# Decoder layer with stick-breaking attention, mLSTM and PEER experts: gate tables beside the next attention, transposed attention weights, and a last pass that ranks one block first

## The chip, the cores and the metric

One NeuronCore of a Trainium2 chip runs the whole layer in one launch. The metric is the device time of that launch in microseconds (us); lower is better. All data are float32.

## The reference, cut to what matters

1024 tokens of width 1024 go through one layer. The kernel works on eight token blocks of 128.

```python
h = layer_norm(x, ln0)
# token mixer: one input projection feeds both branches
z = (q @ k.T) / 8                                   # 8 heads of 64, causal, s < t
w = exp(log_sigmoid(z) + sum_{s'>s} log_sigmoid(-z))  # stick-breaking weights
o_sb = w @ v
o_ml = sigmoid(ml_o) * mlstm(silu(conv(ml_q, ml_k)), ml_v, gates)   # 4 heads of 128
h = layer_norm(ALPHA*h + (sigmoid(g1)*(o_sb @ Wsb) + sigmoid(g2)*(o_ml @ Wml)) @ w_out, ln1)
# PEER: 8 heads; each token takes 16 of 16384 experts per head
s1, s2 = q1 @ k1.T, q2 @ k2.T                       # 128 scores each, per head
v1, i1 = top_k(s1, 16); v2, i2 = top_k(s2, 16)
top_s, pos = top_k(v1[:, None] + v2[None, :], 16)   # out of 256 pairs
idx = (i1*128 + i2)[pos]; gates = softmax(top_s)
ffn = sum_k gates_k * gelu(h . u_tab[idx_k]) * v_tab[idx_k]
h = layer_norm(ALPHA*h + ffn + sigmoid(h @ Wg) * (p @ Wp), ln2)
```

## The kernel before, in words

**Passes.** `BLOCKS` cuts the eight token blocks into three passes, (0, 1), (2, 3, 4) and (5, 6, 7), which `main` (L1141) runs one after the other. A pass is: `pre` (first layer norm and transposes), `project` (L478: keys and values of the attention to DRAM, queries to SBUF), `attention` (L552) merged with `recurrent`, `mlstm` and `gates`, then `branch` (L747: branch projections, output projection, second layer norm), `keys` (L810: the PEER scores and, for each of 16 head halves, the top 16 by `best`, L802), `choose` (L873: pair sums, top 16 pairs, expert numbers, softmax) and `embed` (L839). `pre`, `project` and `embed` of neighbouring passes are merged with these.

**Experts, two ways.** For blocks 0, 1, 2, 5 and 6 class `Experts` (L1063) gathers expert rows: POOL issues one indirect DMA for each of the 128 choices of a block (128 rows of 4 KB into one tile `vr`, `K` = 6 of them, L1078), first from `u` (`first`; VectorE multiplies and sums, L1099), then from `v` (`second`; VectorE adds, L1111). This is 1280 gathers and 1280 VectorE steps over the run. It goes on beside everything from the first `choose` to the end. `first` of one block and `second` of the block before take turns; the loop at L1165 hands one such step to the program for each 1.15 of the cost that `main` yields. Blocks 3, 4 and 7 (`DENSE`) go through all 16384 experts in `dense` (L1009): 128 steps of 24 + 6 matmuls, with gates from tables `Gd` in DRAM that `spread` (L954) makes. `spread` builds one-hot matrices `ohA` and `ohB` on VectorE and ScalarE for four tokens at a time, multiplies them on TensorE and copies the product into `stage` tiles, which SP stores in 16 pieces of 512 KB for each block.

**Attention.** An item is one row (head pair `pr`, token block `j`, head `e` of the pair) by up to four key blocks; rows of blocks 4 to 7 have two items. `s1`: scores (64 of 128 partitions are contracted), then Abs, Exp, Ln and Relu on ScalarE. `s2`: a running sum from the right on VectorE (L597), subtracted from the scale times the scores (L599), then Exp. `s3`: one transpose of each 128x128 piece on TensorE and a copy to `awT`. `s4`: weights by values, 64 output columns (L622). The items go through as a pipeline (L628); `s4` runs when all items of its row are in `done`. `s3` of the next item stands ahead of `s4` in the loop, so a row with two items finds both there at its first call and is computed again at its second.

**Order.** The Tile framework takes the program order as priority and fixes, when the kernel is built, the order in which each engine and each DMA queue works; SP issues nearly all plain DMAs in one such order, POOL the gathers. Tiles of one tag share buffers: `kt` and `vt` of the attention, `stage`, `eq`, `xt` and `mx` share the four of `c4`; `top`, `cv`, `ci`, `self`, `ohA`, `ohB`, `mo`, `mR` and `y` share the seven of `cs`. PSUM has four banks `g`, two `z` (attention scores, `spread`) and two `m` (transposes, attention output, mLSTM).

The lines that set the order around the change:

```python
yield from Merge(attention(o), chain(recurrent(o), Merge(mlstm(o), gates(o))))   # L1148
...
yield from Merge(choose(o, ORDER[i]), chain(embed(o), project(nxt)))             # L1156
...
yield from Merge(choose(o, [t for t in o.tbs if t in DENSE]), embed(o))          # L1161
yield from Merge(choose(o, [t for t in o.tbs if t not in DENSE]), dense(h1s))    # L1163
```

## Time and profile before

| | us |
|---|---|
| median of 3 runs | 3337.85 (3334.37 to 3341.75) |
| the profiled execution, its own time | 3336.88 |
| its span in the trace | 3335.1 |

| from to, us | what runs (besides the gathers, from 403 on) |
|---|---|
| 0 to 400 | pass 0 up to `embed` |
| 402 to 447 | `project` of pass 1 |
| 452 to 765 | attention (to 671), mLSTM (to 765) of pass 1 |
| 748 to 1058 | `branch`, `keys`, `embed` of pass 1; `project` of pass 2 to 1117 |
| 1027 to 1300 | `choose` of blocks 2, 3, 4; `spread` of 3 (1119 to 1194) and 4 (1241 to 1296) |
| 1307 to 1651 | attention (to 1624), mLSTM of pass 2 |
| 1651 to 1898 | `branch`, `keys` of pass 2 (its rankings to 1925) |
| 1898 to 2033 | `embed`; `choose` and `spread` of block 7 |
| 2033 to 2122 | `choose` of blocks 5 and 6, first steps of `dense` |
| 2095 to 3240 | `dense` at an even pace |
| 3240 to 3335 | the gathers' remainder, last layer norms |

PE is the TensorE, DVE the VectorE, ACT the ScalarE, POOL the engine that issues the gathers, SP the one that issues the other DMAs. An x with a number counts instructions; a float32 matmul is two instructions in the trace, a transpose or float32r matmul one.

### The profile page before, as it was taken

To read this page: it belongs to the slowest core of one execution; us is meant where nothing else is said; L and a number is where in the kernel's file an instruction comes from. 1 tells how busy PE (TensorE), PEld (TensorE's weight loads), DVE (VectorE), ACT (ScalarE), POOL (GpSimd) and SP (SyncE) were. 2 spreads that over 40 slices of the span, in tenths; PEclk is the share of its full clock that TensorE was granted. 3 is DMA by queue.
4 is the path that set the end of the run, shared out by engine and by line. 5 is a ranking of instruction groups with operands and counts; after the bars stand their busy time and mean duration, and the time that the engine had idled before them with its cause. 6 is when DMAs were issued, how large, how long until landed. Compare 5 with 4: busy or idle time off the path is not lost.

```text
span 3335.1 us, 38987 instructions
## 1 busy us (share of the span) xinstructions
PE 2974.0 (89%) x12105; PEld 1982.6 (59%) x12105; DVE 2668.9 (80%) x5661; ACT 1101.9 (33%) x2560; POOL 1562.8 (47%) x1313
## 2 busy tenths in 40 slices
PE   7997999969899837999898967899999999999990
PEld 6786654545464535556655545566666666666660
DVE  5635999788699999989887999967776777777788
ACT  4626234430611458556413145111111111111110
POOL 0000156557534553556665343644445555554565
PEclk9998998969999968999899989999999999999995
DMA  6444699989979989898799889999999999999997
GB/s 213 136 146 143 234 350 323 323 281 381 376 271 317 359 273 320 306 340 267 244 373 363 308 303 312 335 361 352 353 346 355 357 353 348 348 355 337 361 329 265
DMA packets 341825, 1035.22 MB, mean 310 GB/s; under 512 B 38512, under 2 KB 95216, under 8 KB 341616
## 3 DMA queue, kind: packets, MB, share of 16 engines
q0 software_dynamic: 184320, 671.17, 56.0%
q1 hardware_dynamic: 157296, 361.55, 30.3%
q8 instruction: 96, 1.57, 0.2%
q14 instruction: 113, 0.93, 0.1%
HBM read 991.17 MB, written 41.42 MB: 310 GB/s over the span
## 4 chain that ended last, share of the span: by engine, by line
PE 67%; DVE 16%; issue 8%; ACT 6%; DMA 2%; POOL 1%; SPq 0%; DVEq 0%; POOLq 0%; ACTq 0%
PE g L274 15%; PE g L1019 13%; PE z L1019 6%; PE m L278 5%; PE m L276 5%; PE m L277 5%; PE g L784 3%; DVE acc L139 3%; PE m L622 3%; ACT ohB L161 2%; PE z L583 2%; DVE vr L139 2%; PE g L276 2%; PE g L278 2%; PE g L277 2%
## 5 line engine op out<-in xcount | busy, mean ns | idle before, releaser
L1079 POOL DMA_INDIRECT vr<-in_u_dram,vidx x640 | 772.9, 1208 | 1013.1 <-DVE V L139 384.5
L1079 POOL DMA_INDIRECT vr<-in_v_dram,vidx x640 | 786.1, 1228 | 729.6 <-DVE acc L139 271.2
L139 DVE SCALAR_TENSOR_TENSOR acc<-vr,w,acc 128x1024 f32<-128x1024 f32 x640 | 817.9, 1278 | 43.6 <-DMA vr<-in_v_dram,vidx 34.4
L139 DVE SCALAR_TENSOR_TENSOR vr<-vr,h1r 128x1024 f32<-128x1024 f32 x640 | 780.0, 1219 | 55.8 <-DMA vr<-in_u_dram,vidx 40.9
L1019 PE MATMUL g<-wf,y 128*128 128x512 f32 x1024 | 462.8, 594 | 14.7 <-DVE y L1043 14.7
L161 ACT ACTIVATE hl<-wf 128x512 fp32r<-128x512 f32 x256 | 160.5, 628 | 765.7 <-PE m L278 599.5
L251 DVE TENSOR_TENSOR hl<-wf,hl 128x512 fp32r<-128x512 f32 x256 | 179.1, 701 | 292.8 <-PE m L277 244.7
L276 PE MATMUL m<-h1s,hl 128*128 128x384 f32 x1024 | 394.7, 385 | 3.5 <-ACT y L161 3.5
L278 PE MATMUL m<-h1s,hl 128*128 128x384 f32 x1024 | 347.8, 340 | 2.7 <-DVE hl L251 2.6
L274 PE MATMUL g<-hT,wf 128*128 128x384 f32 x1024 | 342.7, 489 | 5.8 <-DVE gs L851 3.2
L277 PE MATMUL m<-h1s,hl 128*128 128x384 f32 x1024 | 346.0, 338 | 0.0
L1019 PEld LDWEIGHTS g<-wf,y 128*128 128x128 f32 x1024 | 193.1, 190 | 201.9 <-issue 171.3
L274 PEld LDWEIGHTS g<-hT,wf 128*128 128x128 f32 x1024 | 191.7, 191 | 136.1 <-issue 7.7
L1019 PE MATMUL z<-wf,y 128*128 128x512 f32 x512 | 240.6, 592 | 0.0
L276 PEld LDWEIGHTS m<-h1s,hl 128*128 128x128 f32 x1024 | 194.1, 190 | 34.0 <-issue 29.4
L277 PEld LDWEIGHTS m<-h1s,hl 128*128 128x128 f32 x1024 | 194.1, 190 | 29.2 <-issue 29.2
L278 PEld LDWEIGHTS m<-h1s,hl 128*128 128x128 f32 x1024 | 193.8, 189 | 4.3 <-DVE hl L251 3.3
L987 PE MATMUL z<-ohA,ohB 128*128 128x128 f32 x768 | 137.9, 320 | 47.1 <-ACT ohB L161 18.7
L274 PE MATMUL g<-h1T,wf 128*128 128x384 f32 x512 | 173.1, 493 | 1.5 <-ACT h1T L161 1.4
L1019 PEld LDWEIGHTS z<-wf,y 128*128 128x128 f32 x512 | 97.3, 190 | 122.5 <-issue 122.2
L622 PE MATMUL m<-awT,vt 128*64 128x128 f32 x992 | 150.2, 303 | 18.6 <-ACT awT L173 10.4
L987 PEld LDWEIGHTS z<-ohA,ohB 128*128 128x128 f32 x768 | 112.1, 210 | 74.5 <-ACT ohB L161 53.1
(332 smaller groups left out, 4461.6 us busy)
## 6 DMA issues: line engine op xcount, KB each, us to landing
wf<-in_uE_dram SPq DMA_DIRECT2D x128, 512.0 KB
wf<-in_v_dram SPq DMA_DIRECT2D x128, 512.0 KB
wf<-in_wmain_dram SPq DMA_DIRECT2D x84, 512.0 KB
wf<-in_wgate_dram SPq DMA_DIRECT2D x48, 512.0 KB
wf<-in_wq_dram SPq DMA_DIRECT2D x48, 512.0 KB
Gd<-stage SPq DMA_DIRECT2D x48, 512.0 KB
gp<-Gd SPq DMA_DIRECT2D x32, 768.0 KB
wf<-in_wout_dram SPq DMA_DIRECT2D x24, 512.0 KB
```

The source lines that it names most:

```text
L139: x = getattr(vec, op)(*args, **kw)
L161: x = nc.scalar.activation(o, i, f, **kw)
L251: vec.tensor_tensor(lo, src, hi, op=OP.subtract)
L274: pe.matmul(o, l[0], r[0], start=first, stop=last)
L276: pe.matmul(o, l[0], r[0], start=first, stop=False)
L277: pe.matmul(o, l[0], r[1], start=False, stop=False)
L278: pe.matmul(o, l[1], r[0], start=False, stop=last)
L622: pe.matmul(po[rows, :P], vt[:, lo + s, row["e"] * 64:(row["e"] + 1) * 64], wT[:, s * P:(s + 1) * P], start=i == 0, stop=i == row["nb"] - 1)
L784: pe.matmul(acc, yT[k // 4][:, k % 4, n * P:(n + 1) * P], wo[u][k // 2][:, k % 2, :], start=k == 0, stop=k == 7)
L987: pe.matmul(pg[:, k], B[:, k], A[:, k], start=True, stop=True)
L1019: pe.matmul(acc[d][c], y[:, d * P:(d + 1) * P], wv[:, c * 512:(c + 1) * 512], start=e == 0, stop=e == P - 1)
L1079: pool.indirect_dma_start(out=vr, out_offset=None, in_=use[0], in_offset=bass.IndirectOffsetOnAxis(ap=idx[:, s:s + 1], axis=0))
```

## The change

It does five things.

1. `spread` and what is left of `choose` of pass 1 go beside the attention of pass 2 and no longer only beside `embed` and `project`: classes `Beside` and `Slow`. What is not done when the attention is through follows it (`rest`). The attention's costs are scaled by 2.0, 1.7 and 1.1, so that it is dealt out over more of what it is merged with.
2. Buffers of their own for this: `choose` and `spread` get tag `ch` (4), `stage` and `eq` their tag `stage` (2), and `spread` of blocks 3 and 4 the PSUM banks `m`. `cs` has 5, `c2` 8. To make room, the scale and shift of the last layer norm are loaded into two `vr` buffers each time they are needed, and the descriptor scratch of the gathers shrinks from 8192 to 1024 bytes.
3. In the last pass `keys` ranks only block 7; the scores of 5 and 6 go to DRAM (`scd`). `choose` of block 5 fetches and ranks them beside `spread` of 7, that of block 6 beside `dense`.
4. Attention: the queries are scaled and laid into a tile with zeros for the other head (`qz`), so that scores contract 128 partitions. The scores are copied to SBUF (`zs`). The subtraction and transposition are one PSUM accumulation: a transpose of `zs`, plus a float32 matmul of the running sum with minus identity; Exp comes after, in place of the copy to `awT`. Weights by values run with all 128 columns of the value tile, and half of the result is used.
5. The attention's pipeline has a stage less, and `s4` of item k-2 stands ahead of `s3` of item k-1 in the loop.

```diff
-NC2 = 7
-NCS = 7
+NC2 = 8
+NCS = 5
+NST = 2
+NOH = 4
+SLOW = (2.0, 1.7, 1.1)
+class Slow:
+    def __next__(self):
+        return self.by * next(self.gen)
+class Beside:
+    def along(self, main):
+        now = 0.0
+        for c in main:
+            yield c
+            now += c
+            while self.gen is not None and self.t < now:
+                try:
+                    self.t += next(self.gen)
+                except StopIteration:
+                    self.gen = None
+        self.t = max(0.0, self.t - now)
...
+    nident = T([P, P], F32, "nident")
+    vec.tensor_scalar(nident, ident, -1.0, None, op0=OP.mult)
+    qz = T([P, 2, 2, P], F32, "qz")
+    vec.memset(qz, 0.0)
...
-            t = T([P, D], F32, f"ln2{n}") if i == 2 else c4(f"ln{n}_")
+            t = T([P, D], F32, "vr", K) if i == 2 else c4(f"ln{n}_")
...
         def s1(k):
+            q = row["q"] = qz[:, (pr * o.n + j) % 2, e, :]
+            if first:
+                act.activation(q[rows], o.qT[rows, pr, j * P:(j + 1) * P], AF.Copy, scale=0.125)
             pz = PT("z")
-            pe.matmul(pz[:, :w], o.qT[rows, pr, tsl], kv[pr][0][rows, lo * P:lo * P + w], start=True, stop=True)
+            pe.matmul(pz[:, :w], q, kv[pr][0][:, lo * P:lo * P + w], start=True, stop=True)
...
+            zs = c2("azs")[:, :w]
+            act.copy(zs, pz[:, :w])
...
         def s2(k):
             vec.tensor_tensor_scan(sp[:, ::-1], sp[:, ::-1], rt[:, ::-1], row["carry"], OP.add, OP.add)
             row["carry"] = sp[:, 0:1]
-            vec.scalar_tensor_tensor(rt, pz, 0.125, sp, op0=OP.mult, op1=OP.subtract)
-            act.activation(rt, rt, AF.Exp)
         def s3(k):
             for s in range(n):
-                pe.transpose(pw[:, s * P:(s + 1) * P], rt[:, s * P:(s + 1) * P], ident)
+                c = slice(s * P, (s + 1) * P)
+                pe.transpose(pw[:, c], zs[:, c], ident)
+                pe.matmul(pw[:, c], sp[:, c], nident, start=False, stop=True, skip_group_check=True)
             wT = c2("awT")
-            act.copy(wT[:, :n * P], pw[:, :n * P])
+            act.activation(wT[:, :n * P], pw[:, :n * P], AF.Exp)
         def s4(k):
-                    pe.matmul(po[rows, :P], vt[:, lo + s, row["e"] * 64:(row["e"] + 1) * 64],
-                              wT[:, s * P:(s + 1) * P], start=i == 0, stop=i == row["nb"] - 1)
+                    pe.matmul(po[:, :P], vt[:, lo + s, :], wT[:, s * P:(s + 1) * P],
+                              start=i == 0, stop=i == row["nb"] - 1)
-        for k in range(N + 3):
+        for k in range(N + 2):
+            if 0 <= k - 2 < N:
+                s4(k - 2)
             if k < N:
                 s1(k)
             if 0 <= k - 1 < N:
                 s2(k - 1)
-            if 0 <= k - 2 < N:
-                s3(k - 2)
-            if 0 <= k - 3 < N:
-                s4(k - 3)
+                s3(k - 1)
...
         def ev_q(u):
                 for j in range(n):
-                    best(vec, sc[:, j, :], o.VI[j], head, half)
+                    if j not in o.late:
+                        best(vec, sc[:, j, :], o.VI[j], head, half)
+                if o.late:
+                    a0, a1 = o.late[0], o.late[-1] + 1
+                    dma.dma_start(scd[:, hh, a0:a1, :], sc[:, a0:a1, :])
...
+            if j in o.late:                       # in choose
+                for i in range(2):
+                    late.append(T([P, 8, P], F32, "stage", NST))
+                    dma.dma_start(late[i], scd[:, 8 * i:8 * i + 8, j, :])
+                for hh in range(2 * NH):
+                    best(cvec, late[hh // 8][:, hh % 8, :], o.VI[j], hh // 2, hh % 2)
+                    yield 1.7
...
             if tb in DENSE:
-                yield from spread(tb, vidx, gt)
+                now = spread(tb, vidx, gt)
+                if beside is not None:
+                    now = Merge(now, choose(o, beside))
+                yield from now
...
+        last = tb in BLOCKS[-1]                   # in spread
+        bank, ch = ("z", csel) if last else ("m", cho)
-            st = [c4("stage", (P, 64, 16)) for _ in range(2)]
+            st = [c4("stage") if last else T([P, D], F32, "stage", NST) for _ in range(2)]
...
-            yield from Merge(attention(o), chain(recurrent(o), Merge(mlstm(o), gates(o))))
+            yield from side.along(Merge(Slow(SLOW[i], attention(o)), chain(recurrent(o), Merge(mlstm(o), gates(o)))))
+            yield from side.rest()
...
-                yield from Merge(choose(o, ORDER[i]), chain(embed(o), project(nxt)))
+                side = Beside(Slow(2.0 if i else 1.0, choose(o, ORDER[i])))
+                yield from side.along(chain(embed(o), project(nxt)))
...
-                yield from Merge(choose(o, [t for t in o.tbs if t in DENSE]), embed(o))
+                rest = [t for t in o.tbs if t not in DENSE]
+                yield from Merge(choose(o, [t for t in o.tbs if t in DENSE], rest[:1]), embed(o))
-                yield from Merge(choose(o, [t for t in o.tbs if t not in DENSE]), dense(h1s))
+                yield from Merge(choose(o, rest[1:]), dense(h1s))
...
-    nc = bacc.Bacc("TRN2", target_bir_lowering=False, num_devices=1, dynamic_dma_scratch_size=8192)
+    nc = bacc.Bacc("TRN2", target_bir_lowering=False, num_devices=1, dynamic_dma_scratch_size=1024)
```

## Rows read from the trace of the kernel before

**Rows 1.** The page: busy time and share of the span, by engine.

```profile
PE 2974.0 (89%) x12105; PEld 1982.6 (59%) x12105; DVE 2668.9 (80%) x5661; ACT 1101.9 (33%) x2560; POOL 1562.8 (47%) x1313
```

**Rows 2.** Stretches: length; busy PE, PEld, DVE, ACT, POOL (count); clock; DMA; GB/s.

```profile
400.00:671.00 271.00, 261.48 (x888) 141.23 (x889) 239.59 (x531) 118.55 (x269) 151.97 (x127) 0.95 0.91 326
671.00:765.00 94.00, 64.59 (x267) 48.29 (x268) 80.84 (x145) 24.65 (x60) 59.85 (x49) 0.69 0.81 278
...
1117.00:1307.00 190.00, 108.64 (x573) 85.44 (x573) 183.81 (x431) 123.44 (x379) 90.86 (x73) 0.82 0.87 308
1307.00:1541.00 234.00, 226.91 (x960) 132.13 (x961) 206.06 (x289) 135.12 (x285) 129.40 (x109) 0.96 0.88 315
1541.00:1651.00 110.00, 92.95 (x465) 68.16 (x464) 98.78 (x163) 60.91 (x138) 67.24 (x51) 0.80 0.74 242
...
1977.00:2033.00 56.00, 44.69 (x236) 34.55 (x236) 56.00 (x112) 55.88 (x179) 18.85 (x20) 0.94 0.87 293
2033.00:2095.00 62.00, 40.64 (x161) 29.57 (x160) 57.56 (x230) 17.47 (x34) 25.84 (x21) 0.85 0.87 296
2095.00:3240.00 1145.00, 1144.93 (x4402) 788.78 (x4403) 835.21 (x1310) 200.05 (x366) 603.53 (x477) 1.00 0.96 351
3240.00:3335.00 95.00, 7.92 (x19) 3.23 (x17) 83.34 (x105) 0.00 (x0) 50.19 (x44) 0.55 0.76 277
```

**Rows 3.** The chain in `dense`: start us, length, what; two steps.

```profile
3191.05 3.43 PE g L1019 x8
...
3200.36 3.43 PE g L1019 x8
```

**Rows 4.** The same table as Rows 2, a stretch after `dense`.

```profile
3250.00:3300.00 50.00, 0.00 (x0) 0.00 (x0) 44.45 (x37) 0.00 (x0) 38.80 (x34) 0.50 0.94 339
```

**Rows 5.** Waits, 1117 to 1307: us in total, times, longest.

```profile
PE z L965 <- DVE rs L376: 40.4, 1, 40.4
...
PE z L583 <- DMA kt<-kTd: 6.6, 1, 6.6
```

**Rows 6.** Groups by line: weights by values, of passes 0, 1, 2 in turn.

```profile
L622 PE MATMUL m<-awT,vt 128*64 128x128 f32 x48 | 10.1, 327 | 0.0
L622 PE MATMUL m<-awT,vt 128*64 128x128 f32 x250 | 39.6, 306 | 4.0 <-ACT awT L173 3.4 <-ACT osT L173 0.7
L622 PE MATMUL m<-awT,vt 128*64 128x128 f32 x640 | 92.1, 299 | 13.2 <-ACT awT L173 6.7 <-DVE mkn L691 2.5 <-ACT cqk L161 2.3
```

**Rows 7.** Groups by line, whole span: 128-column matmul, output copy, the subtraction.

```profile
L825 PE MATMUL m<-k,pq 128*128 128x128 f32 x256 | 38.3, 284 | 2.6 <-ACT pq L161 1.8 <-ACT hT L161 0.7
...
L173 ACT ACTIVATE osT<-m 64x128 f32<-64x128 f32 x96 | 25.9, 270 | 66.2 <-PE m L622 61.9 <-issue 3.1 <-ACT art L161 0.3
...
L599 DVE SCALAR_TENSOR_TENSOR art<-z,asp 128x512 f32<-128x512 f32 x48 | 32.8, 683 | 0.7
```

**Rows 8.** PE in order of time: one matmul by itself, twelve in a row.

```profile
1422.46 0.33 PE L585 MATMUL z<-maskz,identr 128*128 128x128 f32 x1
...
1440.14 1.52 PE L622 MATMUL m<-awT,vt 128*64 128x128 f32 x12
```

**Rows 9.** Tile `vr`, VectorE steps: count; ns min/median/max; first and last start, us.

```profile
L139 DVE SCALAR_TENSOR_TENSOR vr<-vr,h1r x640: 1168/1220/1280, 402.6 to 3060.4; 128x1024 f32<-128x1024 f32 x160
L139 DVE DVE_READ_ACCUMULATOR vr<-vr,h1r x640: 70/82/95, 403.7 to 3061.5; 128x1 f32 x160
...
L139 DVE SCALAR_TENSOR_TENSOR acc<-vr,w,acc x640: 1228/1279/1339, 674.4 to 3311.4; 128x1024 f32<-128x1024 f32 x160
```

**Rows 10.** Instructions on tile `sc` alone (`best`, last pass): DVE, ACT.

```profile
1785.00:1925.00 140.00, 59.82 (x382) 7.86 (x16) 0.97 0.89 317
```

**Rows 11.** The chain that ended last: a gather's and a table store's transfer.

```profile
1134.13 10.22 DMA vr<-in_v_dram,vidx
...
1294.60 6.08 DMA Gd<-stage
```

**Rows 12.** DMA queues of the page: packets, MB, time as share of 16 engines.

```profile
q0 software_dynamic: 184320, 671.17, 56.0%
```

More of the change, by code (lines that the diff above doesn't have):

```diff
@@ L98, in __iter__, with __init__, rest @@
             now = max(now, t)
+class Slow:
+    def __init__(self, by, gen):
+        self.by, self.gen = by, gen
+    def __iter__(self):
+        return self
+    def __next__(self):
+        return self.by * next(self.gen)
+class Beside:
+    def __init__(self, gen):
+        self.gen, self.t = gen, 0.0
+    def along(self, main):
[9 more added lines that the diff above has]
+        self.t = max(0.0, self.t - now)
+    def rest(self):
+        if self.gen is not None:
+            yield from self.gen
+            self.gen = None
 class Stream:
@@ L193, in c2, with cho @@
         return sb.tile(list(shape), dt, name=name, tag="c2", bufs=NC2)
+    def cho(name, shape=(P, 512)):
+        return sb.tile(list(shape), F32, name=name, tag="ch", bufs=NOH)
     def csel(name, shape=(P, 512)):
@@ L412, in body @@
     based = dr.tile([S, D], F32, name="based")
+    scd = dr.tile([P, 2 * NH, 3, P], F32, name="scd")
     ND = len(DENSE)
@@ L576, in s1 @@
             row, lo, n, first = work[k]
-            pr, w = row["pr"], n * P
+            pr, j, e, w = row["pr"], row["j"], row["e"], n * P
             if pr + 1 not in kv and pr < 3:
                 load(pr + 1)
-            rows = slice(row["e"] * 64, row["e"] * 64 + 64)
-            tsl = slice(row["j"] * P, (row["j"] + 1) * P)
+            rows = slice(e * 64, e * 64 + 64)
+            q = row["q"] = qz[:, (pr * o.n + j) % 2, e, :]
+            if first:
+                act.activation(q[rows], o.qT[rows, pr, j * P:(j + 1) * P], AF.Copy, scale=0.125)
             pz = PT("z")
-            pe.matmul(pz[:, :w], o.qT[rows, pr, tsl], kv[pr][0][rows, lo * P:lo * P + w], start=True, stop=True)
+            pe.matmul(pz[:, :w], q, kv[pr][0][:, lo * P:lo * P + w], start=True, stop=True)
             if first:
                 pe.matmul(pz[:, w - P:w], identr, maskz, start=False, stop=True, skip_group_check=True)
+            zs = c2("azs")[:, :w]
+            act.copy(zs, pz[:, :w])
             sp = c2("asp")[:, :w]
-            act.activation(sp, pz[:, :w], AF.Abs, scale=0.125)
+            act.activation(sp, pz[:, :w], AF.Abs)
             act.activation(sp, sp, AF.Exp, scale=-1.0)
@@ L814, in keys @@
         o.hold = [c6("hold", (P, 8, P)) for _ in range(2)] if o.i == 0 and o.n == 2 else None
+        o.late = [j for j, tb in enumerate(o.tbs) if tb not in DENSE] if o.i == len(BLOCKS) - 1 else []
         o.VI = [(T([P, 2, NH, 16], F32, "V", 3), T([P, 2, NH, 16], U16, "I", 3)) for _ in range(o.n)]
@@ L871, in body, with choose @@
     cvec, evec = Chain(CD), Chain(ED)
-    def choose(o, tbs):
+    def choose(o, tbs, beside=None):
         for tb in tbs:
@@ L887, in choose @@
             cvec.tensor_scalar(fI[:, 0], fI[:, 0], 128.0, None, op0=OP.mult)
-            cv = csel("cv", (P, NH, NC50))
-            ci = csel("ci", (P, NH, NC50))
+            cv = cho("cv", (P, NH, NC50))
+            ci = cho("ci", (P, NH, NC50))
             def sums(dst, src, of, a0, a1, b0, b1):
@@ L931, in choose @@
                     shape = [P, step, 4, n]
-                    eq = c4("eq")[:, :step * 4 * n].rearrange("p (h k n) -> p h k n", h=step, k=4)
+                    eq = T([P, D], F32, "stage", NST)[:, :step * 4 * n].rearrange("p (h k n) -> p h k n", h=step, k=4)
                     cvec.tensor_tensor(eq, ci[:, h, None, :n].to_broadcast(shape),
@@ L954, in spread @@
     def spread(tb, vidx, gt):
+        last = tb in BLOCKS[-1]
+        bank, ch = ("z", csel) if last else ("m", cho)
         d = DENSE.index(tb)
[L957 to L959 removed]
+        sel = ch("sel", (P, 4, P))
+        f = ch("self", (P, 2, P))
+        ii = ch("seli", (P, 2, P)).bitcast(U32)
         vec.tensor_scalar(ii[:, 0], vidx, 7, None, op0=OP.logical_shift_right)
@@ L963, in spread @@
         by = HOTS
-        pt = PT("z", (P, 4, P))
+        pt = PT(bank, (P, 4, P))
         pe.transpose(pt[:, 0], f[:, 0], ident)
@@ L972, in spread @@
         for q in range(8):
-            st = [c4("stage", (P, 64, 16)) for _ in range(2)]
+            st = [c4("stage") if last else T([P, D], F32, "stage", NST) for _ in range(2)]
+            st = [x.rearrange("p (i t) -> p i t", t=16) for x in st]
             for t in range(q * 16, q * 16 + 16, 4):
-                A, B = (csel(n, (P, 4, P)) for n in ("ohA", "ohB"))
-                pg = PT("z", (P, 4, P))
+                A, B = (ch(n, (P, 4, P)) for n in ("ohA", "ohB"))
+                pg = PT(bank, (P, 4, P))
                 vec.tensor_tensor(A, iota128[:, None, :].to_broadcast([P, 4, P]),
@@ L1048, in dense @@
         back(*todo.pop(0))
-        g, b = ln2
+        g, b = load_ln(2)
         hs = []
@@ L1114, in second @@
             self.flush()
-            g, b = ln2
+            g, b = load_ln(2)
             for _ in layer_norm([acc], g, b):
@@ L1137, in body @@
     ex = Experts()
-    ln2 = []
     def main():
         yield from pre(blks[0])
-        ln2.extend(load_ln(2))
+        side = Beside(iter(()))
         for i, o in enumerate(blks):
```

14 lines of the change are left out of this document (6 added, 8 removed).

## The prediction

> **What bounds the kernel now.** I read the page's busy shares first, then a table by stretch, then the chain of waits, the waits of single stretches, and the groups by line. TensorE is busy 89% of the span [rows 1], and the table says where it is not [rows 2]. `dense` (2095 to 3240) is TensorE alone: 1144.9 of 1145 us. Its step, by the chain, is 9.31 us [rows 3], 128 times, and nothing in the change touches it; what can move is when it starts. After it stand 95 us with TensorE idle, in which the gathers are worked off: VectorE 83 us, 44 gathers [rows 2]. So there are two questions: how much earlier `dense` starts, and how many gathers are then left over for the end.
>
> Ahead of `dense` the worst stretch is 1117 to 1307: TensorE 109 of 190 us, VectorE 184. There `choose` and `spread` of blocks 3 and 4 run almost alone. TensorE waits once for 40.4 us for `spread` of block 4, which waits for `choose` on VectorE, and the attention of pass 2 then waits for `kt` [rows 5], whose buffers `stage` held. From 1307 to 1541 TensorE is full (227 of 234), from 1541 to 1651 (mLSTM at the end) 93 of 110. VectorE is nearly as full all along: 184, 206 and 99 us, together 489 of 534, and it does 73 + 109 + 51 = 233 gathers there (POOL's count) [rows 2].
>
> **Attention's own cost.** On ScalarE the change swaps: Exp moves from the rows to the transposed piece, the copy to `awT` becomes the copy `zs`. New are 64 query copies at 0.27 us (17 us), gone are 32 output copies: there are 96 for 64 rows [rows 7], because a row with two items is computed twice. ScalarE is busy 319 of 534 us in the stretch [rows 2] and has room.
>
> On VectorE the subtraction goes: 0.683 us for 512 columns [rows 7]; pass 2 has 32 of these, 8 of 384 and 8 of 256 columns, by proportion 29 us.
>
> On TensorE each of 288 pieces (24, 96, 168 by pass) gets one more float32 matmul, two instructions. Against that stands the double work: weights by values take 48, 250 and 640 instructions [rows 6], and once over would be 48, 192 and 336. So pass 0 gets 48 more, pass 1 gets 192 - 58 = 134, pass 2 gets 336 - 304 = 32. At 0.15 us (38.3/256) [rows 7] this is 7, 20 and 5 us. Upper bound: if each switch between transpose and matmul costs what a matmul by itself does, 0.33 us against 0.13 in a row [rows 8], two switches a piece add 0.4 us: 10, 38 and 67 us. Nothing in the trace alternates like this; I take the price in a row, since both operands lie ready, and keep the bound for the range. A transpose into a bank before a matmul adds to it has no gain to offer below that.
>
> Weights by values with 128 columns instead of 64: 0.144 us an instruction with 64 (92.1/640) [rows 6], 0.150 with 128 [rows 7], so nothing. The Trainium skill (TensorE: Matmul & The Clock Gate, "LDWEIGHTS (loading the stationary operand)") says that loading goes with the columns, at columns/1.2 ns. By that rule 64 columns more are 53 ns, 336 times 18 us in pass 2, and the forecast would be some 18 us later; the rows do not show it.
>
> **Pass 2, the merged stretch.** TensorE's work is 429 + 5. In the first and last part its clock was granted at 0.82 and 0.80 [rows 2], between idle spells; at full clock these 109 and 93 us would be up to 38 less. I take 10. So 424 us, at the 97% of the full part (227/234) 437 us instead of 534: **97 us** earlier. Bounds: all clock back, 408 us (126 earlier); the dearer switches, 506 us (28 earlier).
>
> What hides the two spreads is this attention. Their ScalarE work is in the 319 us. Their PSUM banks are now `m`, two for transposes, outputs, mLSTM and `spread`; who waits longer there is ScalarE, in fixed order, and behind it the next item's Abs, Exp and Ln. `stage` has two buffers, so after each sixteenth ScalarE's copy waits for the store (6.08 us to land [rows 11]); 16 such waits are 97 us if no other ScalarE work is put between. Between 0 and 97, hidden by 437 - 326 = 111 us of room: I take 0. SP has the stores and the score stores between weight loads, which are five pieces ahead; cover again, cost 0.
>
> VectorE does not fit so well. 489 - 29 = 460 us; gathers 233 x 1.29 us (the mean of 1.279 and of 1.220 + 0.082 [rows 9]) = 301, the rest 159. In 437 us at 97% that leaves 265 us, 205 gathers; today's rate (233/534 = 0.436 per us) gives 191. I take 198: **35 gathers** go to the end. There a gather takes 50/34 = 1.47 us [rows 4], so 51 us come back. `dense` takes no more of them: its 477 gathers go with its DMA share of 0.96 [rows 2], the fullest of these rows.
>
> **Passes 0 and 1.** Pass 0: 7 us later. Pass 1: 400 to 765 has TensorE 261 + 65 of 365 us, the second part at clock 0.69 [rows 2]. The scaled costs deal the attention out over the mLSTM, so the work, 326 + 20 - 10 (half the clock), takes 346 us at 97%: 19, of which I take **15**. Bounds 29 earlier, 33 later with the dearer switches.
>
> **Last pass.** 48 rankings take 59.8 us on VectorE [rows 10], 1.25 each. 32 of them no longer stand ahead of `choose` of block 7; they held it up to 1925, 27 us after `keys` ended on TensorE (1898). But 16 (20 us) and `choose` of block 5 (some 20 us: VectorE outside the gathers, 57.6 - 21 x 1.29 = 30 us for one and a half blocks from 2033 to 2095) now stand beside `spread` of 7, where VectorE (56.0) and ScalarE (55.9 of 56) are full [rows 2]. And 40 us for block 6 take the place of those 30 at the start of `dense`. So between 25 earlier and 15 later; **10** earlier, and 4 gathers fewer (6 us).
>
> **Small things.** Twelve loads for the last layer norm instead of two, and 4.2 MB of scores: 9.4 MB at 351 GB/s [rows 2] are 27 us of DMA, of which I count 6. The layer norm at the end waits for its loads: 3.
>
> **Sum.** 97 - 7 + 15 + 10 = 115 us earlier; back come 51 + 6 + 6 + 3 = 66. The span goes from 3335 to 3286 us. The profiled execution took 1.8 us more than its span, and the median of the runs is 1 us above that: **3288 us**, by itself 3265 to 3310.
>
> **The rivals.**
> - *The gathers keep up* (0.17). Pass 1 has VectorE idle 31 + 13 us [rows 2], `keys` of pass 2 loses 40 us of rankings; if the 39 gathers are caught up there, 57 us do not come back: 3231 us. Against it: one gather order, six buffers.
> - *The spread isn't hidden* (0.18): at half speed `choose` and `spread` of 4 are not through when the attention is, and `rest` puts them ahead of `branch`. Then only the waits of 40.4 and 6.6 us go, 47 in place of 97, with 12 gathers lost (18 us): 3305 us.
> - *Slower* (0.19): in the merged stretch VectorE, in fixed order behind running sums and one-hots that wait for ScalarE, takes fewer gathers. The point: 100 us (115 less the 15 of small costs and last pass) buy 68 gathers, so below (233 - 68)/437 = 0.378 per us all is lost. Beside the spreads the rate was 73/190 = 0.384 and 20/56 = 0.357 [rows 2], with more other VectorE work per us than in the merged stretch. At 0.33, 89 are lost, 131 us: 3368 us.
> - *The gathers' ring gets too short* (0.02): the change cuts its memory to an eighth. A gather is 184320/1280 = 144 packets [rows 12], 9 for each of 16 engines; one took 10.2 us [rows 11], and 1280 between 402.6 and 3311.4 [rows 9] are one in 2.27 us, 4 or 5 under way. Were only four allowed, 2.55 us each would give over 3650 us. By the Trainium skill (DMA: Bandwidth & Descriptors, "Terms" and "SWDGE vs HWDGE vs iDMA") a descriptor is 16 bytes and the rings lie in this memory; 1024 bytes then hold 64, seven gathers of 9, more than the six buffers ask. No run here shows it.
>
> **How the numbers follow.** My forecast has 0.40, the four rivals 0.56, what I haven't thought of 0.04. Faster by over 0.2% (6.7 us, about what can be told from no change): 0.74. Within: 0.07, from between forecast and the slower rival. Slower: 0.19. The range reaches from below the best case, with some clock gained, to near the slower one: 3215 to 3360.
>
> **What the next profile would show.** The first score matmul of pass 2 right behind `project`, near 1120; 576 instructions of weights by values and 64 output copies; the stretch to `branch` some 437 us with TensorE at 97%; `dense` steady near 1980; some 80 gathers after it, over about 150 us. I am wrong if `dense` starts less than 50 us earlier, if the alternating matmuls cost twice a matmul in a row, or if the end isn't longer than now.

## The result, and the profile after

The kernel after takes **3303.34 us** (median, 3299.18 to 3312.72) beside 3336.11 us for the kernel before on the same chip: a ratio of **0.9903** (95% interval 0.9877 to 0.9929). The profiled execution took 3299.18 us, its span is 3297.4 us, 38 less than before. Busy time by engine (PEld is TensorE's loading of stationary operands), from the page of the kernel after:

```profile
PE 2931.9 (89%) x12265; PEld 2026.2 (61%) x12265; DVE 2635.0 (80%) x5567; ACT 1124.2 (34%) x2610; POOL 1587.5 (48%) x1313
```

The shares are those of [rows 1] again, VectorE and TensorE with 34 and 42 us less to do. The table by stretch, whose columns are those of [rows 2], shows what moved:

```profile
715.00:1071.00 356.00, 339.02 (x1111) 191.69 (x1111) 313.02 (x909) 95.78 (x251) 185.49 (x164) 0.98 0.93 344
1071.00:1504.00 433.00, 371.10 (x1812) 271.35 (x1811) 393.86 (x712) 292.99 (x681) 269.53 (x195) 0.90 0.84 305
1504.00:1799.00 295.00, 269.97 (x986) 168.35 (x985) 240.29 (x452) 104.78 (x290) 171.70 (x142) 0.92 0.96 364
1799.00:1969.00 170.00, 116.81 (x443) 87.86 (x442) 168.40 (x546) 84.35 (x222) 62.19 (x50) 0.68 0.79 279
1969.00:2077.00 108.00, 107.23 (x408) 74.03 (x407) 105.50 (x333) 21.24 (x38) 50.46 (x39) 0.98 0.95 337
2077.00:3148.00 1071.00, 1071.00 (x4141) 740.66 (x4140) 767.91 (x1202) 186.92 (x343) 539.99 (x446) 1.00 0.96 351
3148.00:3297.00 149.00, 8.06 (x19) 3.23 (x17) 130.22 (x142) 0.00 (x0) 92.39 (x81) 0.54 0.87 321
```

`project` of pass 2 ends at 1071 (before 1117), the merged stretch at 1504 (1651), `keys` at 1799 (1898). Step 12 of `dense` starts at 2077 (2169), its last steps end at 3148 (3240). Two stretches of the kernel before, to compare with:

```profile
1651.00:1898.00 247.00, 235.46 (x796) 138.40 (x795) 211.19 (x537) 56.47 (x139) 134.88 (x119) 0.97 0.93 345
2169.00:3240.00 1071.00, 1071.00 (x4141) 740.66 (x4140) 766.56 (x1165) 187.08 (x343) 556.74 (x446) 1.00 0.97 350
```

From step 12 on `dense` is the same to the microsecond, 1071 us and 446 gathers, in both kernels. What follows it is longer: 149 us with 81 gathers in place of 95 us with 44 [rows 2]. So 92 us are won ahead of `dense`, and 54 come back behind it.

**Where the 92 us come from.** Ahead of pass 1's first score matmul 4 us are won, in pass 1 up to the end of `project` 42, in the merged stretch 101 (433 for 534). From `branch` to the last `keys` 48 are lost (295 for 247), and from there to step 12 some 7.

**What the merged stretch left over.** Groups of TensorE from 1071 to 1504, running sums and table matmuls:

```profile
L662 PE MATMUL m<-nident,asp 128*128 128x128 f32 x336 | 69.4, 308 | 7.6 <-DVE asp L651 6.5 <-DVE rs L430 0.9
L1062 PE MATMUL m<-ohA,ohB 128*128 128x128 f32 x304 | 54.1, 323 | 17.7 <-DVE ohB L1060 4.9 <-DVE acc L180 4.5 <-ACT ohB L202 3.2
```

Two tables are 512 such instructions, eight for each step of `spread` (64 steps). Only 304 ran here; the other 208, or 26 of the 32 steps of block 4's table, come after 1504. There they hold the chain, shown in order of time (start, length, what):

```profile
1643.14 0.54 ACT stage L214 x2
1643.86 18.78 DMA Gd<-stage
1662.66 0.39 ACT stage L214
1663.10 2.09 PE m L1062 x8
...
1677.20 2.09 PE m L1062 x8
1679.31 0.67 ACT stage L214 x2
1680.08 0.77 PE m L1062 x2
1680.84 0.87 PE m L443 x4
```

This store of a finished sixteenth takes 18.8 us beside weight loads and gathers (6.08 in [rows 11]; another, at 1115.63, took 7.76), `stage` has two buffers, and the transposes of the layer norm (L443) stand on TensorE behind the table's last matmuls.

### The profile page after: what moved, and what is told of

It reads as the page before. It is cut to its first block, busy times and chain, and to the rows that moved or that the text cites. A ratio compares the mean times of both kernels' runs of the same rounds, so it can differ in the third digit from the quotient of the medians.

```text
span 3297.4 us, 39191 instructions
## 1 busy us (share of the span) xinstructions
PE 2931.9 (89%) x12265; PEld 2026.2 (61%) x12265; DVE 2635.0 (80%) x5567; ACT 1124.2 (34%) x2610; POOL 1587.5 (48%) x1313
## 4 chain that ended last, share of the span: by engine, by line
PE 66%; DVE 15%; issue 8%; DMA 4%; ACT 4%; POOL 3%; SPq 0%; DVEq 0%; POOLq 0%; ACTq 0%
PE g L323 15%; PE g L1094 13%; PE z L1094 7%; PE m L327 5%; PE m L325 5%; PE m L326 5%; PE g L838 3%; POOL vr L1154 3%; DVE acc L180 3%; DMA vr<-in_v_dram,vidx 2%; PE g L327 2%; PE g L325 2%; PE g L326 2%; DVE vr L180 2%; PE m L677 1%
## 5 line engine op out<-in xcount | busy, mean ns | idle before, releaser
L1154 POOL DMA_INDIRECT vr<-in_v_dram,vidx x640 | 807.6, 1262 | 668.3 <-DVE acc L180 292.4
L180 DVE SCALAR_TENSOR_TENSOR acc<-vr,w,acc 128x1024 f32<-128x1024 f32 x640 | 819.2, 1280 | 66.8 <-DMA vr<-in_v_dram,vidx 57.6
L300 DVE TENSOR_TENSOR wf<-wf 128x1024 fp32r<-128x1024 f32 x68 | 83.2, 1223 | 76.8 <-ACT wf L202 73.8
L323 PE MATMUL g<-wf,hT 128*128 128x512 f32 x288 | 129.9, 604 | 6.5 <-ACT stored L202 6.5
L323 PEld LDWEIGHTS g<-h1T,wf 128*128 128x128 f32 x512 | 96.6, 193 | 62.3 <-issue 2.4
```

What stands on the lines that cost most here:

```text
L180: x = getattr(vec, op)(*args, **kw)
L300: vec.tensor_tensor(lo, src, hi, op=OP.subtract)
L323: pe.matmul(o, l[0], r[0], start=first, stop=last)
L1154: pool.indirect_dma_start(out=vr, out_offset=None, in_=use[0], in_offset=bass.IndirectOffsetOnAxis(ap=idx[:, s:s + 1], axis=0))
```

## The experiments

**Theory.** The gathers are the 1280 indirect DMAs of expert rows, each followed by a step on VectorE. Two things run side by side from 400 us to the end: the path to and through `dense`, and these gathers. `dense` takes the gathers along at a fixed pace; the rest follow it at 1.46 us each. So time won ahead of `dense` counts only less the gathers that no longer run there. **Rivals:** earlier `dense` counts in full and something behind it eats it up; or single parts of the change bring the gain or spoil it.

The first eight kernels undo or alter one part each. Their places in `dense`, counted from the trace (a gather is done when VectorE's step on its `vr` starts):

| kernel | us | step 12 at | gathers by then | step 127 at | left then | from there to the end | 25 + 1.46 x left |
|---|---|---|---|---|---|---|---|
| before | 3336.1 | 2169 | 785 | 3239 | 49 | 96 | 97 |
| after | 3303.3 | 2077 | 750 | 3147 | 86 | 151 | 151 |
| e1_once | 3332.3 | 2141 | 775 | 3208 | 60 | 113 | 113 |
| e2_flat | 3308.8 | 2123 | 773 | 3193 | 60 | 114 | 113 |
| e3_brisk | 3328.6 | 2189 | 807 | 3259 | 27 | 65 | 64 |
| e4_seven_alone | 3303.4 | 2077 | 748 | 3142 | 88 | 155 | 153 |
| e7_shared | 3329.1 | 2065 | 722 | 3132 | 117 | 196 | 196 |
| e8_ahead | 3345.5 | 2227 | 817 | 3295 | 17 | 52 | 50 |
| e9_short | 3306.3 | 2038 | 720 | 3107 | 117 | 200 | 196 |
| e12_rows | 3382.5 | 2152 | 744 | 3219 | 92 | 162 | 159 |

The last column was fitted to these rows, and it holds to 5 us in every one. It also fits three kernels that it was not fitted to, further down: e5_pace with 39 left (83 us, formula 82), e10_pace46 with 5 (36, formula 32) and e11_pace_before with 4 (30, formula 31). From step 12 to 127 `dense` takes 1065 to 1071 us and 441 to 447 gathers in all ten.

A place is read from one execution each. The kernel after, e5_pace, e6_cut and e10_pace46 work through the same instructions in the same order up to step 12, and yet it came at 2077, 2089, 2097 and 2080, with 750 gathers done each time. So a place ahead of `dense` is good to some 20 us; the count of gathers is steadier.

**The double work alone taken out of the kernel before.**

```diff
-            if len(row["done"]) < row["n"]:
+            if len(row["done"]) < row["n"] or row.get("out"):
                 return
+            row["out"] = True
```

> The kernel before, with one edit: weights by values of a row with two items are computed once instead of twice. My theory: in passes 1 and 2 TensorE sets the pace, so taking away some 58 and 304 of its instructions at 0.15 us (9 and 45 us) lets dense start 40 to 50 us earlier; about half comes back as gathers left for the end, so 3310 to 3322 us. The first score matmul of pass 2 stays where it was against the end of its projection. Rival: ScalarE's copies and the order of the pipeline set the pace in the attention, not TensorE's double work; then under 8 us are gained. A second question: pass 1 became 45 us shorter in the changed kernel. If the double work is its cause, most of that shows here; if the dealing-out of the attention over the mLSTM is, 10 us or less.

3332.3 us, ratio 0.997 (0.9958 to 0.9983), between the two expectations. In the profiled execution, at 3322.6 the fastest of six, `project` of pass 2 ends 10 us earlier and `dense` 31, but 11 more gathers are left, 16 us of the 31. The edit takes out 416 instructions, not 362 (below). At most these 10 of pass 1's 42 us are the double work.

**The attention not dealt out.**

```diff
-SLOW = (2.0, 1.7, 1.1)
+SLOW = (1.0, 1.0, 1.0)
```

> The changed kernel with all three attention factors set to 1.0, so that the attention is dealt out over less of what it is merged with. If the dealing-out made pass 1 shorter, most of its 45 us go again: the stretch from the first score matmul of pass 1 to the end of its mLSTM grows from 266 to 290 to 310 us, and the time is 10 to 25 us above the changed kernel's 3303. If it was the work taken out of the attention, the stretch stays within 8 us and so does the time.

3308.8 us, ratio 0.9906 (0.9889 to 0.9923). `project` of pass 2 ends at 1117 again, as in the kernel before: pass 1's gain hangs on the dealing out. It is worth almost nothing: `dense` ends 47 us later than in the kernel after, but 26 more gathers are done by then (38 us).

**The table dealt out faster.**

```diff
-                side = Beside(Slow(2.0 if i else 1.0, choose(o, ORDER[i])))
+                side = Beside(Slow(1.0, choose(o, ORDER[i])))
```

> The changed kernel with choose and spread of pass 1 dealt out twice as fast beside the attention of pass 2 (factor 1.0 instead of 2.0). My theory: what was lost behind the merged stretch (48 us from branch to keys of pass 2) is the remainder of the table of block 4, which stands ahead of the transposes of the second layer norm and waits for its stores with two stage buffers. With it done inside the attention, the stretch from the last output projection matmul to the first query projection of keys falls from 57 to some 25 us, dense starts 20 to 40 us earlier, about half comes back at the end: 3280 to 3295 us. Rival: the loss is a DMA share of 0.98 and a full VectorE there; then the stretch stays near 50 us and the time within 8 us of 3303.

3328.6 us, ratio 0.9963 (0.9948 to 0.9977). From the last output product to the first query projection it is 15 us in place of 51 (14 in the kernel before), as expected, and `branch` to `keys` takes 246 us again. But the time did not follow: the table now ran ahead of `project`, which ended at 1160, and the merged stretch took 506 us. Columns as above:

```profile
1071.00:1160.00 89.00, 73.66 (x255) 44.83 (x255) 69.28 (x107) 35.35 (x93) 54.85 (x43) 0.82 0.99 361
1160.00:1666.00 506.00, 388.70 (x1917) 284.84 (x1916) 462.68 (x817) 296.28 (x740) 326.34 (x239) 0.86 0.88 315
1666.00:1912.00 246.00, 233.32 (x779) 136.54 (x778) 190.97 (x314) 62.51 (x141) 148.31 (x123) 0.97 0.97 366
```

The pace of 2.0 buys an early attention and pays with a table that is not through in time.

**Block 5's `choose` moved from the table of block 7 to `dense`.**

```diff
-                yield from Merge(choose(o, [t for t in o.tbs if t in DENSE], rest[:1]), embed(o))
+                yield from Merge(choose(o, [t for t in o.tbs if t in DENSE]), embed(o))
...
-                yield from Merge(choose(o, rest[1:]), dense(h1s))
+                yield from Merge(choose(o, rest), dense(h1s))
```

> The changed kernel, but choose of block 5 runs beside dense with that of block 6 and no longer beside the table of block 7. My theory: the table's 104 us become 60, dense's first steps come 35 to 45 us earlier but go slower than 9.3 us while VectorE does 80 us of choose; even pace is reached 10 to 30 us earlier, half of it comes back at the end: 3288 to 3300 us. Rival: the same VectorE work stands ahead of the even pace either way, so it begins within 8 us of the changed kernel's and the time stays within 6 us of 3303.

3303.4 us, ratio 0.9886 (0.9862 to 0.9909). The order on the engines stayed practically the same: block 5's ranking still ran at 1861 to 1906. The edit did not do what it was for, and what this ranking costs beside the table of block 7 was not measured.

**The last 48 gathers left out**, the ends of block 6's second half.

```diff
-            for s in range(P):
+            for s in range(P - 48 if tb == 6 else P):
```

> The kernel after, with the last 48 gathered rows of the last block's second half left out (those rows hold whatever was there). If the tail is nothing but the gathers that dense left over, at 1.47 us each, the span falls by 48 x 1.47 = 71 us to about 3227, time about 3232, and dense stays where it is. If the tail is held by something else behind dense (the norm, the output), it falls by less than 20 us, to 3283 or more.

3239.5 us, 64 us less; in the profiled execution `dense` ended 20 us later than in that of the kernel after. The table by stretch, last steps of `dense` and what follows:

```profile
2097.00:3167.00 1070.00, 1070.00 (x4139) 740.17 (x4138) 767.08 (x1202) 187.03 (x343) 539.31 (x446) 1.00 0.96 351
3167.00:3248.00 81.00, 9.09 (x22) 3.71 (x20) 69.63 (x94) 0.00 (x0) 37.96 (x33) 0.58 0.77 283
```

`dense` is as long as ever, and 38 gathers stand behind it for 81 us, where 25 + 1.46 x 38 is 80. The tail is gathers and some 25 us of norm and output.

**The table's buffers shared again.**

```diff
-NC4 = 4
+NC4 = 6
-NCS = 5
+NCS = 9
-        return sb.tile(list(shape), F32, name=name, tag="ch", bufs=NOH)
+        return sb.tile(list(shape), F32, name=name, tag="cs", bufs=NCS)
-                    late.append(T([P, 8, P], F32, "stage", NST))
+                    late.append(c4("stage", (P, 8, P)))
...
-                    eq = T([P, D], F32, "stage", NST)[:, :step * 4 * n].rearrange("p (h k n) -> p h k n", h=step, k=4)
+                    eq = c4("stage")[:, :step * 4 * n].rearrange("p (h k n) -> p h k n", h=step, k=4)
...
-            st = [c4("stage") if last else T([P, D], F32, "stage", NST) for _ in range(2)]
+            st = [c4("stage") if last else c4("stage") for _ in range(2)]
```

> The kernel after, with the gate table's own buffers given back: its one-hot tiles take turns with the attention's softmax tiles again (nine of one kind instead of four and five), its stages with the attention's (six of one kind instead of two and four). If the own buffers carry the gain, the table of block 4 and the attention beside it wait for each other's buffers, the merged stretch of 433 us grows by 40 us or more, and at some 0.4 us of time for each us by which dense comes later the time is 3320 or more. If the merging carries it, the time is 3295 to 3312.

3329.1 us, ratio 0.9965 (0.9952 to 0.9977): 26 us worse, but not for the expected reason. The merged stretch is only 14 us longer (447), `branch` to `keys` is 33 shorter (262), and step 12 comes 12 us earlier, within the scatter above. What is lost is gathers, 28 by step 12. POOL's waits (engine, line, what for; us, times, longest) in the merged stretch, of this kernel first, then of the kernel after:

```profile
POOL vr L1154 <- DVE acc L180: 58.3, 31, 8.5
POOL vr L1154 <- DVE vr L180: 40.6, 23, 5.6
```

```profile
POOL vr L1154 <- DVE acc L180: 38.8, 27, 3.3
...
POOL vr L1154 <- DVE vr L180: 24.4, 14, 3.4
```

With shared buffers the issue of gathers waits 36 us longer for VectorE's steps to free a `vr`. That the one-hots, waiting for a buffer in VectorE's fixed order, hold these steps up is my reading; no run shows it by itself.

**The spreading undone, all else kept.**

```diff
-                side = Beside(Slow(2.0 if i else 1.0, choose(o, ORDER[i])))
-                yield from side.along(chain(embed(o), project(nxt)))
+                yield from Merge(choose(o, ORDER[i]), chain(embed(o), project(nxt)))
```

> The kernel after, with the table of each block dealt out beside the next block's entry and projections alone, as before, and not beside its attention too; own buffers and transposed attention stay. If the spreading carries the gain, the merged stretch goes back from 433 towards 534 us, the stretch from the output product to the last keys shrinks back by 48 us, dense ends some 50 us later, and at 0.4 us for each the time is 3320 to 3335. If the transposed attention and the buffers carry it, 3295 to 3312.

3345.5 us, ratio 1.0009 (0.9996 to 1.0021): nothing is left of the gain, and the time lies above both expectations. Transposed attention, own buffers and the new last pass are together worth nothing without the spreading. Stretches from 1157 on:

```profile
1157.00:1400.00 243.00, 131.12 (x467) 98.67 (x465) 220.19 (x446) 111.51 (x313) 159.53 (x113) 0.57 0.89 320
1400.00:1735.00 335.00, 299.15 (x1459) 214.71 (x1459) 298.62 (x465) 192.99 (x431) 215.00 (x169) 0.92 0.88 314
1735.00:1981.00 246.00, 232.15 (x774) 135.94 (x775) 190.46 (x284) 52.22 (x132) 140.68 (x116) 0.97 0.94 353
```

The bare stretch of tables is back (TensorE 131 of 243 us, at a granted clock of 0.57, near the lower of its two levels), `branch` to `keys` is 246 us again, and `project` lasts up to 1157. The bare stretch is 243 us long for 190 in the kernel before [rows 2]; that buffers cut for the spreading cost time without it is possible, and no run separates it. `dense` ends 149 us later than in the kernel after, not 50; the 69 gathers done meanwhile give 101 us back.

**The remainder of block 4's table left out.** Of the 32 steps the last 20 are not computed; their stores stay.

```diff
+            if tb == 4 and q >= 3:
+                st = kept
+            kept = st
             for t in range(q * 16, q * 16 + 16, 4):
+                if tb == 4 and q >= 3:
+                    break
```

> The kernel after, with the last 20 of the 32 spread steps of block 4's table left out (their stages store the values of an earlier step). In the kernel after 27 of these 32 steps run behind the end of pass 2's mLSTM, and the stretch from the start of the branch to the last keys is 295 us instead of 247. If it is these steps that lengthen it, it shrinks by 20/27 of the 48 us, some 35 us, dense ends as much earlier, and at 0.385 us of time for each the time falls by 13 us, to about 3290. If something else lengthens it, the stretch stays within 10 us of 295 and the time within 5 us of 3303. If an earlier dense were worth its full time, 3268.

3306.3 us, ratio 0.9897 (0.9879 to 0.9915). First the place, then the price:

```profile
1512.00:1759.00 247.00, 236.66 (x823) 140.53 (x822) 178.27 (x350) 63.02 (x164) 133.89 (x110) 0.98 0.97 370
```

The stretch is 247 us to the microsecond of the kernel before, so the work of 20 of the 26 late steps accounts for the 48 us (their stores stay, so what part of it was waiting for a store is not shown). e3_brisk, where the table was through in time, has 246. `dense` starts 39 us earlier, and yet the time doesn't fall: 30 gathers fewer are done by then (110 for 142 in this stretch alone), 44 us. That is the theory at its sharpest. My 13 us rested on a smaller loss of gathers.

**The attention of the kernel before, all else kept.** The whole function is put back; its core:

```diff
-                pe.transpose(pw[:, c], zs[:, c], ident)
-                pe.matmul(pw[:, c], sp[:, c], nident, start=False, stop=True, skip_group_check=True)
+                pe.transpose(pw[:, s * P:(s + 1) * P], rt[:, s * P:(s + 1) * P], ident)
```

> The kernel after with the attention of the kernel before (scores subtracted and exponentiated by rows, rows of two items computed twice); spreading, own buffers and last pass stay. If the transposed attention takes part in the gain, VectorE's 29 us of subtractions in pass 2 come back in a stretch where it is 90% busy, the merged stretch of 433 us takes 455 to 470 us, fewer gathers are done in each microsecond of it, and the time is 3312 to 3330. If VectorE has room there, the merged stretch stays within 10 us of 433 and the time is 3297 to 3309.

3382.5 us, ratio 1.0124 (1.0104 to 1.0144): **slower than the kernel before**. `project` of pass 2 ends 29 us later, which wasn't expected, and the merged stretch takes 479 us, more than the 455 to 470 expected, with hardly a gather more (198 for 195). The stretch, then two of its waits:

```profile
1100.00:1579.00 479.00, 403.32 (x1813) 265.15 (x1814) 420.00 (x765) 327.42 (x709) 258.00 (x198) 0.88 0.80 282
```

```profile
DVE asp L647 <- ACT asp L202: 26.3, 16, 4.2
ACT art L202 <- DVE art L649: 21.1, 19, 4.4
```

In the kernel after the first is 8.0 us in 5 waits, and the second can't exist: the subtraction that sent each row from ScalarE to VectorE and back is gone. That this detour, in a stretch where VectorE also makes one-hots in a fixed order, is what costs so much is my reading: the edit brings back the double work too, and TensorE is busy 403 us there for 371. Beside spread tables no run has one without the other (e1_once, without them, has 10 us for the double work).

**Are the gathers bound to their pace in `dense`?** TensorE is full there and the DMA share 0.96, but both kernels take the same 446 gathers there, about 3.9 a step, which points to the built-in order. So step e of `dense` is put behind a gather on VectorE, 4.3 to a step:

```diff
-                vec.tensor_tensor(y3[:, c], y3[:, c], gp[e // 8 % 2][c][:, :, e % 8, :], op=OP.mult)
+                x = vec.tensor_tensor(y3[:, c], y3[:, c], gp[e // 8 % 2][c][:, :, e % 8, :], op=OP.mult)
+            need = 750 + int(4.3 * (e - 12))
+            if e > 12 and need < len(ex.done):
+                order(x, ex.done[need])
...
-            f(vr)
+            self.done.append(f(vr))
```

> The kernel after, with one more rule for the order: the last block's dense step e is put behind gather number 750 + 4.3(e - 12), so that by step 127 some 1244 rows have been fetched, where the kernel after has 1194. If the gathers' pace in dense is only the order in which the kernel was built, 50 gathers leave the tail at 1.47 us each, dense keeps its step, and the time falls by about 73 us to some 3230. If a gather beside dense cannot be had faster than one in 2.4 us, the steps stretch to 4.3 x 2.39 = 10.3 us instead of 9.3, dense ends some 110 us later, and the time rises to 3320 to 3345.

3280.6 us, ratio 0.9822 (0.9806 to 0.9839), between the two expectations. Then 4.6 to a step (same edit, another number), and 4.3 from 785 on in the kernel before:

> The kernel after, with dense step e behind gather number 750 + 4.6(e - 12), so that all but the last few rows are fetched when dense ends; with 4.3 per step the time was 3280.6, dense took 43 us longer for 51 gathers more (0.8 us each) and 34 were left. If that price holds, 34 gathers move into dense for 27 us and leave the tail, where they cost 1.5 us each, and the time falls to 3250 to 3265. If dense is now full, so that a gather costs as much beside it as alone, the time stays at 3275 to 3285.

> The kernel before with the same rule, dense step e behind gather number 785 + 4.3(e - 12), which has 1279 of 1280 rows fetched by step 127 instead of 1231. If the pace of the gathers beside dense is a matter of order alone and has nothing to do with the change, the 48 rows cost some 0.8 us each beside dense instead of 1.5 us behind it, and the time falls by 25 to 40 us, to 3296 to 3312. If the kernel before was full already, it stays within 8 us of 3337.

With 4.6: **3264.5 us**, ratio 0.9778 (0.9762 to 0.9795), the fastest that does all the work. The kernel before with 4.3: 3306.4 us, ratio 0.9901 (0.9884 to 0.9917). `dense` from step 12 and what follows it, in this order: 4.3, 4.6, before with 4.3:

```profile
2089.00:3201.00 1112.00, 1085.39 (x4151) 743.01 (x4149) 830.54 (x1254) 182.30 (x343) 579.23 (x496) 1.00 0.97 362
3201.00:3278.00 77.00, 5.40 (x8) 2.03 (x8) 64.84 (x90) 0.00 (x0) 34.83 (x31) 0.55 0.77 280
```

```profile
2080.00:3237.00 1157.00, 1097.08 (x4152) 740.92 (x4150) 871.58 (x1289) 181.59 (x343) 611.47 (x525) 0.99 0.97 365
3237.00:3263.00 26.00, 6.14 (x8) 2.37 (x8) 20.36 (x55) 0.00 (x0) 0.00 (x0) 0.57 0.21 85
```

```profile
2166.00:3281.00 1115.00, 1089.54 (x4152) 741.69 (x4150) 821.63 (x1216) 180.68 (x343) 612.32 (x490) 1.00 0.96 359
3281.00:3305.00 24.00, 4.18 (x10) 1.44 (x8) 20.50 (x56) 0.00 (x0) 0.00 (x0) 0.63 0.22 87
```

In these stretches VectorE takes 495 and 530 gathers of the kernel after, where it took 445. A gather more beside `dense` so costs 41/50 = 0.8 us of it at 4.3 and 86/85 = 1.0 us at 4.6 on average, behind it 1.46. The last ones are dearer: from 4.3 to 4.6 it is 45/35 = 1.3 us. Accordingly, from step 12 to the end the kernel after takes 1221 us, 1189 with 4.3 and 1183 with 4.6: the second step brings 6 us there, and the rest of the 16 us between the two times lies ahead of step 12, where their work is the same.

The rule is independent of the change: on the kernel before it brings 32 us at 4.3, on the kernel after 23 at 4.3 and 39 at 4.6. At 4.3 each, the change is worth 26 us instead of 33; with all gathers taken along, which needs 4.3 in the kernel before and 4.6 in the kernel after, it is worth 42. At both paces the weights of `dense` come late. Waits for them in the kernel with 4.3 and with 4.6:

```profile
ACT hl L202 <- DMA wf<-in_uE_dram: 162.9, 50, 14.3
ACT hl L202 <- DMA wf<-in_uE_dram: 208.7, 50, 9.6
```

In the kernel after ScalarE waited for TensorE instead:

```profile
ACT hl L202 <- PE m L326: 727.4, 200, 6.2
```

## Why the prediction was right or wrong, step by step

**The merged stretch** was forecast at 437 us and took 433; 198 gathers were forecast and POOL issued 195. The hit was luck, for the reason was not the one given. TensorE was to do the work of both tables there at 97%; it is busy 371 of 433 us, because 26 steps of block 4's table fell out of the stretch. VectorE is the fuller engine, 394 of 433. Which of the two ends the stretch isn't settled.

**From `branch` to `keys`** the forecast had no loss, and that is the step that failed. I took 0 for the waits for the stores of `stage`, between 0 and 97, "hidden by 437 - 326 = 111 us of room", and looked only at whether a copy waits, not at what the table's pace of 2.0 leaves over. It is the mechanism of the second rival, the spread that isn't hidden. e9_short shows that 20 of these 26 steps make up the 48 us. The two stretches together win 101 - 48 = 53 us of the 97; that rival had 47, and 3305 us. That its time is closer to the measured one than mine is partly chance, though: it lost 12 gathers, where 35 were lost, and had no more than 15 us from pass 1.

**Pass 0 and 1.** 7 later and 15 earlier were forecast, 4 and 42 earlier came. With the attention not dealt out all of this is gone, with the attention by rows 29 of it. The 42 lie beyond my bound of 29. I had counted on half of the lost clock alone; that the scaled costs lay the attention beside pass 1's mLSTM, which ends at 714 instead of 765, I had taken at a third of its worth.

**Last pass.** 10 earlier was forecast, 7 later came. `spread` of block 7 took 104 us instead of 56 [rows 2], VectorE without a gap, the clock close to its lower level:

```profile
1862.00:1966.00 104.00, 60.73 (x252) 52.63 (x251) 104.00 (x362) 66.17 (x196) 30.00 (x28) 0.56 0.70 239
```

The prediction named this collision with 15 later as its bound. e4_seven_alone was to show which part of it is block 5's ranking and left that open.

**The sum ahead of `dense`**: forecast 97 - 7 + 15 + 10 = 115, measured 101 - 48 + 4 + 42 - 7 = 92. The span misses its forecast by 11 us only (3297 for 3286): behind `dense` 12 us less came back than the 66 forecast. That it is so near is in part luck: the 48 us lost and the 17 missed in the last pass stand against 38 more than forecast from passes 0 and 1.

**Gathers given back.** 39 fewer were forecast by the time of `dense`; 35 it was (750 for 785 by step 12). The price of 1.47 us [rows 4] is the fitted 1.46. Forecast 57 us of gathers, measured 54. This term, which eats up half of the gain and more, was right in its price and its sum. By stretch it was not: POOL issued 37 fewer in the merged stretch (35 forecast), but also 12 fewer in pass 1, 23 more from `branch` to `keys` and 12 fewer from there to step 12, and these three cancel by chance.

**`dense` takes no more of them** was read from its DMA share of 0.96 and was wrong, though not by much: e10_pace46 gets 85 more gathers into it at 1.0 us each, the last 35 at 1.3. For the forecast it made no difference, as the change doesn't alter this order; as a reading of the profile it hid 39 us.

**Attention's own cost** was small, as worked out, with 576 instructions of weights by values and 64 output copies. But the double work taken out was larger than I had it. My 250 and 640 [rows 6] came from windows that cut off the ends of passes 1 and 2; over the whole passes it is 272 and 672. So pass 1 gets 192 - 80 = 112 more instructions and pass 2 none, where I had 134 and 32, some 8 us less. The pages agree: 48 + 112 = 160 more on TensorE, 12265 for 12105 [rows 1]. Groups by line, whole span:

```profile
L677 PE MATMUL m<-awT,vt 128*128 128x128 f32 x576 | 86.8, 299 | 6.6 <-ACT awT L202 3.1 <-ACT msw L202 0.9 <-ACT stage L214 0.7
...
L214 ACT ACTIVATE osT<-m 64x128 f32<-64x128 f32 x64 | 17.2, 269 | 67.6 <-PE m L677 62.8 <-PE g L323 3.9
```

Over the whole pass 2 an instruction with 128 columns takes 49.73/336 = 0.148 us, with 64 it took 97.74/672 = 0.145. The Trainium skill (TensorE: Matmul & The Clock Gate, "LDWEIGHTS (loading the stationary operand)") gives a load columns/1.2 ns, an estimate of 53 ns more; the trace has 3. Transposes and matmuls in turn, TensorE in order of time:

```profile
1334.48 0.27 PE L661 MATMUL m<-ident,azs 128*128 128x128 f32 x1
1334.59 0.39 PE L662 MATMUL m<-nident,asp 128*128 128x128 f32 x2
1334.81 0.27 PE L661 MATMUL m<-ident,azs 128*128 128x128 f32 x1
```

The granted clock is 1.00 here. A piece of three instructions starts every 0.33 us, 0.11 each, below the 1.52/12 = 0.13 of twelve in a row [rows 8]. Over all of pass 2 the two lines take 78.0 us for 504 instructions, 0.155 us each: no dearer switch.

**The other rivals.** The gathers did not keep up (35 lost). The slower one, VectorE in fixed order taking fewer gathers, did not come, but e12_rows goes its way: its rate in the merged stretch is 198/479 = 0.413 per us against 195/433 = 0.450 (the rival's limit was 0.378), and the kernel is slower than before. The attention of the kernel after keeps it away; the prediction had counted that as 29 us of VectorE's work and no more. The gathers' ring is not too short: 81 gathers in the tail at 1.46 us match the 1.47 of [rows 4] with the eightfold memory.

## What to carry to other kernels

Where two streams share a chip to the end, time won for one counts only less what the other did meanwhile: here minus x us plus 1.46 us for each gather that no longer fits, so that 39 us won in e9_short were worth nothing. A DMA share of 0.96 beside a full TensorE doesn't say that no transfer fits any more; ask for more by order alone and see what the other stream pays, and what the last ones cost. Parts of a change can be worth nothing, or less, until they meet: all of it but the new attention is 1.2% slower than before, all of it but the spreading brings nothing, and together they win 1%.

## What the runs showed of the hardware

A gather of 512 KB costs 1.46 us by itself, but on average only 0.8 to 1.0 us of a `dense` that seemed full at 351 GB/s (e5_pace, e10_pace46), and 1.3 us for the last ones; the same stretch moved 365 GB/s when more was asked of it. One 512 KB store of a table took 18.8 us among weight loads and gathers, where one took 6.1 in the kernel before. Twice the stationary columns, or a transpose between two matmuls, left the price of an instruction on TensorE as it was, 0.15 us in the group and 0.11 at full clock.
